# Expert loop of a hybrid block: weights in 1-MB transfers, a written TensorE order, a silu gate, and 34 weight places

## The chip, the cores and the metric

The kernel runs on one core of one Trainium2 chip. The metric is the device time of one launch in microseconds (us), the median of several runs. The engines are TensorE (PE in the rows; PEld is its weight load), VectorE (DVE), ScalarE (ACT), GpSimd (POOL) and SyncE (SP), which only issues DMAs here. Sixteen DMA engines carry every transfer of the core.

## The reference, cut to what matters

One layer over 1,024 positions of width 1,024. The first two thirds of the kernel's time (projections, a short convolution, attention, output projection) are not touched. The change is in the mixture of experts at the end: each token goes to 2 of 32 experts.

```python
comb = jnp.sum(jax.nn.one_hot(e_idx, N_EXPERTS, dtype=jnp.float32)
               * w_k[..., None], axis=-2).astype(h.dtype)
out = jnp.zeros_like(h)
for e in range(N_EXPERTS):
    a = jax.nn.silu(h @ w_gate[e]) * (h @ w_up[e])
    out = out + comb[..., e:e + 1] * (a @ w_down[e])
```

`D_MODEL` is 1024 and `D_EXPERT` 256, so an expert has 3 MB of float32 weights. The block's output is `x + gate2 * out`.

## The kernel before, in words

**One expert.** The loop in `moe` goes through 32 experts in a fixed order, each with up to 104 token rows (`CAP`). For expert number n, GpSimd gathers the rows of its tokens into a tile `xg` (L1198, an indirect DMA); TensorE transposes them in 8 instructions into `xT` (L1214); ScalarE and VectorE copy them out as `xf` (two eighths, plain float32) and `xh` and `xl` (six eighths, as a high and a low part; L1215 to L1217). `front` then makes `gu`, gate and up side by side, from 4 weight pieces: 4 matmuls with the first piece whole (L1224), 18 with the other three, each split into a high part by ScalarE (L1185) and a low part by VectorE (L1189). The gate is `sg`: a sigmoid on ScalarE, then two VectorE multiplications (L1237, L1238). TensorE transposes it (`aT`, L1241), and it is split in turn (`ah`, `al`). `back` makes `yp` from the 2 down pieces with 12 matmuls (L1260 to L1262), VectorE multiplies it by the token weights and by `gate2` into `y` (L1263), and GpSimd adds the rows to the output in DRAM by an indirect, accumulating DMA (L1264, here called the scatter).

**Order.** `front(n)` calls `back(n-1)` before the gate of n. Each engine takes its instructions in the order in which a scheduler, at build time, put them; `issue_after` forces one place in that order. Before the change, nothing forces TensorE's order in the loop. On the chip each engine works strictly in its order and waits on semaphores.

**Weights.** An expert has 6 pieces of 512 KB (128 partitions of 4 KB): 192 pieces in all, fetched by SyncE in order (L1105). `plan_room` lists the places. Thirty-one are filled ahead (`fill`); of them 27 are used again in a ring, `wphi` being given back to the split parts. `pa0` (also `stage`), `pa1`, `H0`, `H1` and `H2` are blocks of 4 neighbouring places; the others stand alone. When a piece is used up, `piece_done` issues the load of the next one into the next place of the ring. A fourth block under the name `H` is `xg`, 4 gather tiles, so gather n+4 waits for the transposes of n. `y` has 3 tiles.

**The start and the end of the loop.** The token tables (`tabi`, the rows of each expert; `tabw`, their weights) are made by routing code just ahead. Four GpSimd products `twts` (L997) belong to `tabw`. The scatters of the four neighbouring experts may be in flight together, since these have no token in common; only the last one waits for all. A loop for overflowing experts follows and has nothing to do with these inputs.

Of the kernel before, what the change touches and what calls it, by code (L numbers as in the profile page):

```python
# [56 lines left out]
def plan_room():  # L57
# [5 lines left out]
    fill = [t for t in RAW_ROOM for _ in range(ROOM[t])]  # L63
    ring = [t for t in fill if t not in SPLIT_ROOM]
    free = [(0.0, t) for t in SPLIT_ROOM if t not in fill for _ in range(ROOM[t])]
# [21 lines left out]
class Builder:  # L87
# [978 lines left out]
    def raw_begin(self):  # L1066

        a = self.a
        self.order = [8 * g + e for e in range(8) for g in range(4)]
        gu = [[a["w_gu"][e, q] for q in range(4)] for e in self.order] + [[]]  # L1070
        wd = [[]] + [[a["w_d"][e, q] for q in range(2)] for e in self.order]
        self.pieces = [p for g, w in zip(gu, wd) for p in g + w]
        self.fill, self.ring, self.pairs = plan_room()
        self.raws, self.nraw, self.nsplit, self.npiece, self.blocks = [], 0, 0, 0, {}
        self.raw_fill("wpraw", "wphi", "wplo", "pa0")

    def raw_fill(self, *slots):

        while self.nraw < len(self.fill) and self.fill[self.nraw] in slots:
            self.raw_next()  # L1080

    def raw_rest(self, late):
# [5 lines left out]
        self.xg, self.rows = [xg[:, i, :] for i in range(4)], {}  # L1088
# [4 lines left out]
        self.raw_fill("H2")  # L1093

    def raw_next(self):
        if self.pieces:
            self.raws.append(self.raw_load(self.pieces.pop(0)))

    def raw_load(self, src):

        i = self.nraw
        self.nraw += 1
        fill, ring = self.fill, self.ring
        raw = self.piece_tile(fill[i] if i < len(fill) else ring[(i - len(fill)) % len(ring)], list(src.shape), F32)
        self.nc.sync.dma_start(out=raw, in_=src)  # L1105
        return raw

    def piece_tile(self, slot, shape, dt):

        if slot in ("pa0", "pa1", "H0", "H1", "H2"):  # L1110
            if slot not in self.blocks:
                if slot == "pa0":
                    t = self.stage_tile[:, 0:4 * D].rearrange("p (n d) -> p n d", n=4)
                else:
                    pool, tag = (self.hp, "H") if slot[0] == "H" else (self.mgp, slot)
                    t = pool.tile([P, 4, D], dt, name=slot, tag=tag)
                self.blocks[slot] = [t, 0]
            t, n = self.blocks[slot]
            self.blocks[slot][1] = (n + 1) % 4
            t = t[:, n, :]  # L1120
            return t.rearrange("p (k n) -> p k n", k=2) if len(shape) == 3 else t
        pool = self.wk if slot == "mhi" else self.wp if slot in ("wphi", "wplo") else self.mgp
        return pool.tile(shape, dt, name=slot, tag=slot, bufs=ROOM[slot])

    def moe(self):
        tc, nc, a = self.tc, self.nc, self.a
        with ExitStack() as ctx:
# [7 lines left out]
            self.gate2 = gate2  # L1135
            self.adds = []
            job = None
            for n, e in enumerate(self.order):
# [16 lines left out]
            with tc.For_i(0, cnt, 1) as i:  # L1155
# [6 lines left out]
                job = self.front(NE, P, tabo[:, 0:1],  # L1162
                                 [a["w_gu"][ds(e, 1), q].rearrange("o p k n -> p (o k) n") for q in range(4)])
                self.back(NE, P, *job, tabo[:, 1:2].bitcast(F32),
                          [a["w_d"][ds(e, 1), q].rearrange("o p n -> p (o n)") for q in range(2)])
# [5 lines left out]
    def piece_done(self, src):  # L1171
# [3 lines left out]
        if src is None and (i >= len(self.fill) or self.fill[i] in self.ring):  # L1175
            self.raw_next()
# [27 lines left out]
    def front(self, n, m, idx, wgu_src, between=None):  # L1204
# [12 lines left out]
        nc.vector.tensor_tensor(out=xl, in0=ps[:, nw:KC, 0:m], in1=xh.bitcast(F32), op=ALU.subtract)  # L1217
        gu = pp.tile([P, 512], F32, name="gu", tag="gu")[0:m, :]
        for q in range(4):
            ks = range(2 * q, 2 * q + 2)  # L1220
            if q in WHOLE:
                w = self.whole(wgu_src[q])
                for kc in ks:
                    nc.tensor.matmul(gu, xf[:, kc, :], w[:, kc % 2, :], start=(kc == 0), stop=False)  # L1224
                self.piece_done(wgu_src[q])
                continue
            w = self.piece(wgu_src[q])
            for kc in ks:
                wh, wl = (t[:, kc % 2, :] for t in w)
                nc.tensor.matmul(gu, xh[:, kc - nw, :], wh, start=(kc == 0), stop=False)  # L1230
                nc.tensor.matmul(gu, xh[:, kc - nw, :], wl, start=False, stop=False)
                nc.tensor.matmul(gu, xl[:, kc - nw, :], wh, start=False, stop=(kc == KC - 1))
        s = wk.tile([P, 256], F32, name="sg")[0:m, :]
        if between:
# [99 lines left out]
```

## Time and profile before

| what | value |
|---|---|
| time, median of 3 runs | 1232.86 us (1231.57 to 1232.97) |
| the profiled execution, its own time | 1234.61 us |
| its span, first to last instruction | 1232.6 us |
| TensorE busy in the span | 1124.1 us (91%) |
| TensorE's mean granted clock | 0.973 of full speed |
| first product of the expert loop | 848.5 us into the span |
| first product of the last expert (number 31) | 1200.49 us |

The span is what the rows below are counted in; the execution's own time is 2.0 us longer, and lies 1.75 us above the median. The stretch of about 385 us from 848 on is the expert loop, and 32 us of it are behind the last expert's first product.

### The profile page before, as it was taken

What the parts mean: (1) busy time and instruction counts of PE and PEld (TensorE: products, weight loads), DVE (VectorE), ACT (ScalarE), POOL (GpSimd) and SP (SyncE); (2) the same over time, 40 slices, a digit from 0 to 9 for tenths busy, and PEclk for the clock granted to TensorE, in tenths of its full rate; (3) what the DMA queues carried; (4) which work ended last, traced back from release to release, by engine and by line L of the source; (5) the groups of instructions that cost most, each with busy time, mean ns of one, the idle gap of its engine ahead of it and who ended that gap; (6) DMA issues with size and microseconds to landing.
All of it is one profiled execution on the core that took longest, in us unless ns stands there. A gap on an engine that the chain in (4) does not pass through costs nothing. (4 is left out here: it accounts for less than half of the span.)

```text
span 1232.6 us, 15836 instructions
## 1 busy us (share of the span) xinstructions
PE 1124.1 (91%) x5428; PEld 884.5 (72%) x5428; DVE 814.6 (66%) x1505; ACT 558.8 (45%) x939; POOL 327.9 (27%) x307
## 2 busy tenths in 40 slices
PE   4889999999999989999999999985999998898893
PEld 4878888898997767788888888873666665565562
DVE  5956565565565655645666656867888887586782
ACT  5544553543543664333232233334665565464560
POOL 4440320230230210000000102645465444243211
PEclk9999999999999999999999999996999999899897
DMA  8514123122211426655656564387999999999941
GB/s 306 187 53 126 35 78 81 48 65 71 71 52 43 112 78 201 206 182 175 216 190 205 188 253 188 121 323 218 293 297 294 285 310 272 323 302 293 317 151 25
DMA packets 75219, 222.93 MB, mean 181 GB/s; under 512 B 12897, under 2 KB 17601, under 8 KB 75138
## 3 DMA queue, kind: packets, MB, share of 16 engines
q1 hardware_dynamic: 64162, 200.64, 49.5%
q0 software_dynamic: 9824, 17.09, 6.5%
q10 hardware_dynamic: 1152, 4.19, 0.9%
q8 instruction: 43, 0.70, 0.2%
q14 instruction: 38, 0.31, 0.1%
HBM read 201.57 MB, written 26.58 MB: 185 GB/s over the span
## 5 line engine op out<-in xcount | busy, mean ns | idle before, releaser
L1198 POOL DMA_INDIRECT xg<-d_h,tabi x32 | 78.7, 2459 | 153.3 <-PE xT L1214 92.4
L436 POOL TENSOR_SCALAR p<-p,su 128x128 f32<-128x128 f32 (+3 forms) x64 | 48.6, 765 | 229.4 <-DVE su L435 208.4
L498 PE MATMUL gps<-hhi,wphi 128*128 128x512 f32 x256 | 101.6, 397 | 0.6 <-ACT wphi L99 0.6
L500 PE MATMUL gps<-hhi,wplo 128*128 128x512 f32 x256 | 101.3, 396 | 0.5 <-DVE wplo L100 0.5
L99 ACT ACTIVATE wphi<-wpraw 128x1024 fp32r<-128x1024 f32 x42 | 44.6, 1063 | 125.0 <-PE gps L499 47.5
L499 PE MATMUL gps<-hlo,wphi 128*128 128x512 f32 x256 | 101.2, 395 | 0.0
L450 DVE TENSOR_TENSOR pl<-pT,ph 128x512 fp32r<-128x512 f32 (+1 forms) x96 | 51.2, 552 | 46.8 <-ACT ph L449 46.4
L498 PE MATMUL cps<-hhi,wphi 128*128 128x512 f32 x192 | 77.4, 403 | 2.4 <-ACT wphi L99 2.0
L1264 POOL DMA_INDIRECT out_dram<-y,tabi x32 | 59.0, 1842 | 66.5 <-DVE y L1263 47.2
L499 PE MATMUL cps<-hlo,wphi 128*128 128x512 f32 x192 | 76.3, 398 | 0.0
L500 PE MATMUL cps<-hhi,wplo 128*128 128x512 f32 x192 | 75.1, 399 | 0.3 <-DVE wplo L100 0.3
L449 ACT ACTIVATE ph<-pT 128x512 fp32r<-128x512 f32 (+1 forms) x96 | 44.5, 489 | 64.3 <-PE pT L446 58.9
L100 DVE TENSOR_TENSOR wplo<-wpraw,wphi 128x1024 fp32r<-128x1024 f32 x42 | 51.4, 1224 | 31.3 <-ACT wphi L99 31.3
L186 DVE SCALAR_TENSOR_TENSOR adaw<-adaw,cb 128x1024 f32<-128x1024 f32 x32 | 39.2, 1225 | 47.1 <-DMA adaw<-in_w_ada_dram 47.1
L1185 ACT ACTIVATE wphi<-H 128x1024 fp32r<-128x1024 f32 x48 | 50.2, 1058 | 42.8 <-issue 30.3
L316 PE MATMUL qkvp<-wplo,hhi 128*128 128x384 f32 x192 | 65.7, 342 | 0.7 <-DVE wplo L100 0.7
L315 PE MATMUL qkvp<-wphi,hhi 128*128 128x384 f32 x192 | 65.4, 348 | 0.8 <-ACT wphi L99 0.8
L317 PE MATMUL qkvp<-wphi,hlo 128*128 128x384 f32 x192 | 65.2, 340 | 0.0
L100 DVE TENSOR_TENSOR wplo<-waraw,wphi 128x768 fp32r<-128x768 f32 (+2 forms) x37 | 38.0, 1027 | 40.0 <-ACT wphi L99 39.1
L816 POOL IOTA slots<- 128x128 f32 x1 | 0.2, 244 | 226.9 <-DVE adaw L186 226.9
L434 ACT ACTIVATE p<-p,m 128x128 f32<-128x128 f32 (+3 forms) x64 | 49.4, 773 | 22.9 <-DVE m L431 13.1
L498 PEld LDWEIGHTS gps<-hhi,wphi 128*128 128x128 f32 x256 | 48.1, 188 | 12.7 <-ACT wphi L99 1.1
(473 smaller groups left out, 3211.2 us busy)
## 6 DMA issues: line engine op xcount, KB each, us to landing
H<-in_w_gu_dram SPq DMA_DIRECT2D x53, 512.0 KB
adaw<-in_w_ada_dram SPq DMA_DIRECT2D x32, 512.0 KB
wpraw<-in_w_g_dram SPq DMA_DIRECT2D x30, 512.0 KB
H<-in_w_d_dram SPq DMA_DIRECT2D x30, 512.0 KB
stage<-in_w_gu_dram SPq DMA_DIRECT2D x22, 512.0 KB
wplo<-in_w_gu_dram SPq DMA_DIRECT2D x18, 512.0 KB
pa<-in_w_gu_dram SPq DMA_DIRECT2D x18, 512.0 KB
ld<-in_w_ada_dram SPq DMA_DIRECT2D x16, 512.0 KB
```

What stands on the lines that cost most here:

```text
L100: (lo_eng or nc.vector).tensor_tensor(out=lo, in0=raw, in1=hi.bitcast(F32), op=ALU.subtract)
L315: nc.tensor.matmul(ps, hi[:, kc, sl], wh, start=(kc == 0), stop=False)
L316: nc.tensor.matmul(ps, hi[:, kc, sl], wl, start=False, stop=False)
L317: nc.tensor.matmul(ps, lo[:, kc, sl], wh, start=False, stop=(kc == KC - 1))
L434: nc.scalar.activation(pr, pr, AF.Exp, bias=m[:, b:b + 1], scale=-1.0, accum_out=su)
L450: nc.vector.tensor_tensor(out=pl[:, off:], in0=tp[:, off:], in1=ph[:, off:].bitcast(F32), op=ALU.subtract)
L498: nc.tensor.matmul(ps, wh, hi[:, kc, :], start=(kc == 0), stop=False)
L499: nc.tensor.matmul(ps, wh, lo[:, kc, :], start=False, stop=False)
L500: nc.tensor.matmul(ps, wl, hi[:, kc, :], start=False, stop=(kc == KC - 1))
L1185: nc.scalar.activation(hi, raw, AF.Copy)
L1198: self.gather = self.nc.gpsimd.indirect_dma_start(out=x[0:m, :], out_offset=None, in_=self.d_h2, in_offset=bass.IndirectOffsetOnAxis(ap=id ...
L1264: ins = nc.gpsimd.indirect_dma_start(out=self.out, out_offset=bass.IndirectOffsetOnAxis(ap=idx, axis=0), in_=y, in_offset=None, bounds_che ...
```

## The change

Six things change together in the expert loop. (1) Two neighbouring places of a block are filled by one 1-MB transfer, and `layout` puts both pieces of it side by side, so that a partition gets 8 KB in one row. Single places still get 512 KB. (2) There are 34 places, 30 of them in the ring: `xg` keeps 2 gather tiles and gives the other half as block `H3`, and the place `wkx` stands where the third `y` tile was. A load is issued when the place, or both places, of it are used up. (3) `in_turn` forces TensorE's order: the first piece's products of n, the gate transposes of n-1, the other products of n, all 8 row transposes of n+1, `back(n-1)`. (4) The gate is one ScalarE instruction (Silu) and one VectorE instruction, which also applies the token weights; `y` then multiplies by `gate2` alone. (5) Gather n+1 is written in `between`, and gather n waits for the transposes of n-2. (6) The last scatter waits only for the one four before it, like the others. Numbers of lines move: 1105 to 1106 (1-MB) and 1131 (512 KB), 1198 to 1248, 1214 to 1265, 1224 to 1291, 1241 to 1316, 1263 to 1338, 1264 to 1339.

```diff
-ROOM = {"mhi": 3, "row": 2, "mh": 1, "ml": 1, "wpraw": 3, "wphi": 4, "wplo": 4,
-        "pa0": 4, "pa1": 4, "H0": 4, "H1": 4, "H2": 4}
-RAW_ROOM = ("wphi", "pa0", "wpraw", "wplo", "pa1", "H0", "H1", "H2")
-SPLIT_ROOM = ("mhi", "row", "mh", "ml", "wphi")
+
+RAW_ROOM = (("wphi", 4), ("pa0", 4), ("wpraw", 2), ("wplo", 4), ("pa1", 4), ("H0", 4), ("H1", 4), ("H2", 4),
+            ("H3", 2), ("wpraw", 1), ("wkx", 1))
+SPLIT_ROOM = {"mhi": 3, "row": 2, "mh": 1, "ml": 1, "wphi": 4}
+BLOCKS = {"pa0": 4, "pa1": 4, "H0": 4, "H1": 4, "H2": 4, "H3": 2}
+ROOM = SPLIT_ROOM | {"wpraw": 3, "wplo": 4, "wkx": 1}
...
-        gu = [[a["w_gu"][e, q] for q in range(4)] for e in self.order] + [[]]
-        wd = [[]] + [[a["w_d"][e, q] for q in range(2)] for e in self.order]
-        self.pieces = [p for g, w in zip(gu, wd) for p in g + w]
+        gu = [[a["w_gu"][e, q] for q in range(2)] for e in self.order] + [[]]
+        wd = [[]] + [[a["w_d"][e]] for e in self.order]
+        self.twos = [p for g, w in zip(gu, wd) for p in g + w]
...
-        self.xg, self.rows = [xg[:, i, :] for i in range(4)], {}
+        self.blocks["H3"] = [xg, 0]
+        self.xg, self.rows = [xg[:, i, :] for i in (2, 3)], {}
...
+        self.raw_fill("H2", "H3", "wpraw")
+
+    def raw_next(self, limit):
+
+        i, two = self.nraw, self.slot_of(self.nraw) in BLOCKS
+        if i >= NCHUNK or i + two >= limit:
+            return False
+        src = self.twos[i // 2]
+        if two:
+            t, n = self.block(self.slot_of(i))
+            self.nc.sync.dma_start(out=t[:, n:n + 2, :].rearrange("p a n -> p (a n)"),
+                                   in_=src if len(src.shape) == 2 else src.rearrange("p k n -> p (k n)"))
+            self.raws += [self.view(t[:, n + b, :], src) for b in range(2)]
+            self.blocks[self.slot_of(i)][1] = (n + 2) % BLOCKS[self.slot_of(i)]
+            self.nraw += 2
+        else:
+            self.raws.append(self.raw_load(self.half(src, i % 2)))
+        return True
...
+            self.raw_fill("wkx")
...
+            self.turn = None
+            xs = self.tokens(0, CAP, self.tabi[:, self.order[0]:self.order[0] + 1])
...
+                following = []
+
+                def before():
+                    if n > 0:
+                        jobs[-1] += self.turned(n, CAP, acts)
+
+                def between():
+                    if n < NE - 1:
+                        f = self.order[n + 1]
+                        following.append(self.tokens(n + 1, CAP, self.tabi[:, f:f + 1]))
+                    if n > 0:
+                        self.back(n - 1, CAP, *jobs[-1], [None] * 2)
+                acts = self.front(n, CAP, *xs[1:], self.tabw[:, e:e + 1], [None] * 4, before, between)
+                jobs.append([xs[0]])
+                xs = following[0] if following else None
+            self.back(NE - 1, CAP, *jobs[-1], *self.turned(NE - 1, CAP, acts), [None] * 2)
...
-        if src is None and (i >= len(self.fill) or self.fill[i] in self.ring):
-            self.raw_next()
+        if src is None and self.slot_of(i) in self.ring:
+            self.nfree += 1
+            while self.raw_next(len(self.fill) + self.nfree):
+                pass
...
-            x = self.xg[n % 4]
+            x = self.xg[n % 2]
...
-        for kc in range(KC):
-            nc.tensor.transpose(ps[:, kc, 0:m], x[0:m, kc * P:(kc + 1) * P], self.ident[0:m, 0:m])
+        with self.in_turn(n) as turn:
+            for kc in range(KC):
+                turn(nc.tensor.transpose(ps[:, kc, 0:m], x[0:m, kc * P:(kc + 1) * P], self.ident[0:m, 0:m]))
         nc.scalar.activation(xf, ps[:, 0:nw, 0:m], AF.Copy)
         nc.scalar.activation(xh, ps[:, nw:KC, 0:m], AF.Copy)
         nc.vector.tensor_tensor(out=xl, in0=ps[:, nw:KC, 0:m], in1=xh.bitcast(F32), op=ALU.subtract)
+        return idx, nw, xf, xh, xl
...
+    @contextmanager
+    def in_turn(self, n):
+
+        def turn(ins):
+            self.turn = ins if n < NE else None
+        with ExitStack() as ctx:
+            if n < NE and self.turn is not None:
+                ctx.enter_context(self.tc.issue_after(self.turn.ins))
+            yield turn
...
-                for kc in ks:
-                    nc.tensor.matmul(gu, xf[:, kc, :], w[:, kc % 2, :], start=(kc == 0), stop=False)
+                with self.in_turn(n) as turn:
+                    for kc in ks:
+                        turn(nc.tensor.matmul(gu, xf[:, kc, :], w[:, kc % 2, :], start=(kc == 0), stop=False))
                 self.piece_done(wgu_src[q])
+                if before and q == 0:
+                    before()
...
+            with self.in_turn(n) as turn:
+                for kc in ks:
+                    wh, wl = (t[:, kc % 2, :] for t in w)
+                    nc.tensor.matmul(gu, xh[:, kc - nw, :], wh, start=(kc == 0), stop=False)
+                    nc.tensor.matmul(gu, xh[:, kc - nw, :], wl, start=False, stop=False)
+                    turn(nc.tensor.matmul(gu, xl[:, kc - nw, :], wh, start=False, stop=(kc == KC - 1)))
         s = wk.tile([P, 256], F32, name="sg")[0:m, :]
+        nc.scalar.activation(s, gu[:, 0:256], AF.Silu)
+        nc.vector.scalar_tensor_tensor(s, gu[:, 256:512], comb[0:m, :], s, op0=ALU.mult, op1=ALU.mult)
         if between:
...
-        nc.scalar.activation(s, gu[:, 0:256], AF.Sigmoid)
-        nc.vector.tensor_tensor(out=s, in0=gu[:, 0:256], in1=s, op=ALU.mult)
-        nc.vector.tensor_tensor(out=s, in0=gu[:, 256:512], in1=s, op=ALU.mult)
...
-        return idx, ah, al
...
+        return ah, al
...
-        comb = comb[0:m, :]
         wd = [self.piece(wd_src[q]) for q in range(2)]
-        y = wk.tile([P, D], F32, name="y", bufs=3 if n < NE else 1)[0:m, :]
+        y = wk.tile([P, D], F32, name="y", bufs=2 if n < NE else 1)[0:m, :]
         yp = pp.tile([P, D], F32, name="yp", tag="yp", bufs=1)[0:m, :]
...
-        nc.vector.scalar_tensor_tensor(y, yp, comb, self.gate2[0:m, :], op0=ALU.mult, op1=ALU.mult)
+        with self.in_turn(n) as turn:
...
+        nc.vector.tensor_tensor(out=y, in0=yp, in1=self.gate2[0:m, :], op=ALU.mult)
...
-        if n < NE - 1:
+        if n < NE:
             befores = self.adds[-4:-3] or self.out_init
             self.adds.append(self.unordered(ins, self.adds[-3:], befores, "experts of other groups have other tokens"))
-        elif n == NE - 1:
-            self.after(ins, self.adds[-4:], "the last sum waits for all")
+        else:
...
-        "w_gu": np.concatenate([f["w_gate"][0], f["w_up"][0]], axis=2).reshape(NE, 4, 2, P, 512)
+        "w_gu": np.concatenate([f["w_gate"][0], f["w_up"][0]], axis=2).reshape(NE, 2, 4, P, 512)
         .transpose(0, 1, 3, 2, 4),
-        "w_d": f["w_down"][0].reshape(NE, 2, P, D),
+        "w_d": f["w_down"][0].reshape(NE, 2, P, D).transpose(0, 2, 1, 3).reshape(NE, P, 2 * D),
```

The first place at which the order moves is GpSimd's queue at the start of the loop. Before (`xg` is a gather, `twts` a product of the token weights, `d_tab` a record for overflowing experts):

```order
L1198 DMA xg<-d_h_95,tabi 104x1024
L997 TENSOR_TENSOR twts<-tval_7686,fae_7560 128x96 x2
L997 TENSOR_TENSOR twts<-tval_7686,fbe_7569 128x96 x2
L1198 DMA xg<-d_h_95,tabi 104x1024 x3
L1025 DMA d_tab<-rec_90,idx_89 65536x2 x2
L1048 IOTA jidx 128x1
```

After the change:

```order
L999 TENSOR_TENSOR twts<-tval_7675,fae_7549 128x96 x2
L999 TENSOR_TENSOR twts<-tval_7675,fbe_7558 128x96 x2
L1248 DMA xg<-d_h_95,tabi 104x1024 x2
L1050 IOTA jidx 128x1
L1248 DMA xg<-d_h_95,tabi 104x1024 x3
L1027 DMA d_tab<-rec_90,idx_89 65536x2 x2
```

The first gather stood ahead of the four `twts` products and now stands behind them; two of the gathers stand ahead of the first `jidx`.

The second place is TensorE's queue around one change of experts, in the steady part of the loop. Before:

```order
L1260 MATMUL yp<-row,ah 104x512
L1261 MATMUL yp<-mhi,ah 104x512
L1262 MATMUL yp<-row,al 104x512
L1214 MATMUL xT<-ident,xg 128x104 x6
L1241 MATMUL aT<-ident,sg 128x104 x2
L1224 MATMUL gu<-stage,xf 104x512 x2
L1230 MATMUL gu<-row,xh 104x512
L1231 MATMUL gu<-mhi,xh 104x512
L1260 MATMUL yp<-wphi,ah 104x512
L1261 MATMUL yp<-mhi,ah 104x512
L1232 MATMUL gu<-row,xl 104x512
L1230 MATMUL gu<-row,xh 104x512
```

After the change, where the rows left out are ten more `yp` products like their neighbours:

```order
L1301 MATMUL gu<-mh,xh 104x512
L1302 MATMUL gu<-wphi,xl 104x512
L1265 MATMUL xT<-ident,xg 128x104 x8
L1335 MATMUL yp<-mhi,ah 104x512
...
L1335 MATMUL yp<-mhi,ah 104x512
L1336 MATMUL yp<-ml,ah 104x512
L1337 MATMUL yp<-mhi,al 104x512
L1291 MATMUL gu<-wplo,xf 104x512 x2
L1316 MATMUL aT<-ident,sg 128x104 x2
L1300 MATMUL gu<-row,xh 104x512
L1301 MATMUL gu<-row,xh 104x512
```

The last 6 row transposes stood directly ahead of the gate transposes and of the first products that use them. Now all 8 stand ahead of the 12 `yp` products, and the gate transposes stand behind the first products of the next expert.

The third place is SyncE's queue in the same part. Before (128x1024 is a piece of 512 KB):

```order
L1105 DMA H_7526<-in_w_d_dram 128x1024 x2
L1105 DMA H_7526<-in_w_gu_dram 128x1024 x2
L1105 DMA H_7536<-in_w_gu_dram 128x1024
L1105 DMA H_7521<-in_w_gu_dram 128x1024
L1105 DMA H_7536<-in_w_d_dram 128x1024 x2
L1105 DMA stage<-in_w_gu_dram 128x1024 x3
L1105 DMA H_7536<-in_w_gu_dram 128x1024
L1105 DMA wpraw<-in_w_d_dram 128x1024 x2
L1105 DMA wpraw<-in_w_gu_dram 128x1024
```

After the change (128x2048 is 1 MB; L1131 issues the single places):

```order
L1106 DMA pa_7414<-in_w_gu_dram 128x2048
L1106 DMA H_7515<-in_w_d_dram 128x2048
L1106 DMA H_7518<-in_w_gu_dram 128x2048 x2
L1106 DMA H_7524<-in_w_d_dram 128x2048
L1106 DMA xg<-in_w_gu_dram 128x2048
L1131 DMA wpraw<-in_w_d_dram 128x1024
L1106 DMA H_7524<-in_w_gu_dram 128x2048
L1131 DMA wkx<-in_w_d_dram 128x1024
L1106 DMA stage<-in_w_gu_dram 128x2048
```

Most pairs of pieces are now one entry; the pieces come in the same sequence.

## Rows read from the trace of the kernel before

**Rows 1.** The page: span and busy time.

```profile
span 1232.6 us, 15836 instructions
...
PE 1124.1 (91%) x5428; PEld 884.5 (72%) x5428; DVE 814.6 (66%) x1505; ACT 558.8 (45%) x939; POOL 327.9 (27%) x307
```

**Rows 2.** Busy time by stretch of the expert loop; columns in the first line.

```profile
core 0: us, PE busy (x) PEld busy (x) DVE busy (x) ACT busy (x) POOL busy (x), PEclk, DMA share, GB/s
880.00:920.00 40.00, 37.33 (x163) 24.70 (x163) 32.98 (x38) 23.82 (x35) 28.11 (x14) 1.00 1.02 307
...
1040.00:1080.00 40.00, 31.78 (x117) 19.81 (x116) 25.48 (x30) 18.68 (x27) 12.11 (x6) 0.83 0.98 308
...
1120.00:1160.00 40.00, 32.02 (x133) 20.41 (x132) 26.44 (x30) 19.10 (x27) 11.98 (x6) 0.91 0.95 294
...
1185.00:1190.00 5.00, 4.08 (x25) 3.01 (x24) 4.79 (x7) 4.21 (x7) 0.00 (x0) 1.00 0.21 53
```

**Rows 3.** Waits of TensorE, 860 to the end: us in total, times, longest.

```profile
PE gu L1224 <- ACT xf L1215: 18.7, 27, 1.2
PE aT L1241 <- DVE sg L1238: 15.8, 14, 5.3
```

**Rows 4.** Waits of SyncE's DMA queue from 800 on: us in total, times, longest.

```profile
SPq L1105 <- DMA H<-in_w_gu_dram: 51.8, 33, 3.1
...
SPq L1105 <- DVE mhi L1189: 20.0, 15, 2.8
```

**Rows 5.** The DMA view of 820 to 845, in 40 slices of 0.625 us.

```profile
GB/s 419 419 426 406 406 419 420 419 413 419 420 406 216 229 315 184 275 269 295 406 419 426 413 420 419 420 413 157 0 0 0 0 0 0 0 13 0 66 59 157
```

**Rows 6.** Timeline of SyncE's queue: start, us to the last issue of the group, x issues.

```profile
904.31 0.33 SPq L1105 DMA_DIRECT2D H<-in_w_gu_dram  x1
...
1162.99 7.17 SPq L1105 DMA_DIRECT2D H<-in_w_gu_dram  x4
1171.73 4.19 SPq L1105 DMA_DIRECT2D H<-in_w_d_dram  x4
1176.83 0.33 SPq L1105 DMA_DIRECT2D H<-in_w_gu_dram  x1
```

**Rows 7.** Indirect DMAs issued from 904 to 1163: count, median us to landing.

```profile
xg<-d_h,tabi POOLq DMA_INDIRECT x23, 10.6
out_dram<-y,tabi POOLq DMA_INDIRECT x23, 10.9
```

**Rows 8.** Timeline of GpSimd at the start of the loop.

```profile
841.24 1.30 POOL L1198 DMA_INDIRECT xg<-d_h,tabi  x1 [1.37 <-DVE ee L1007]
842.58 0.67 POOL L997 TENSOR_TENSOR twts<-tval,fae 128x96 bf16<-128x96 bf16 x2
843.22 1.71 POOL L997 TENSOR_TENSOR twts<-tval,fbe 128x96 bf16<-128x96 bf16 x2
```

**Rows 9.** Timeline of TensorE: first product of expert 5 and of expert 15.

```profile
902.31 0.68 PE L1224 MATMUL gu<-H,xf 128*104 128x512 f32 x1 [0.93 <-ACT xf L1215]
...
1009.15 0.68 PE L1224 MATMUL gu<-stage,xf 128*104 128x512 f32 x1 [0.45 <-ACT xf L1215]
```

**Rows 10.** Groups of instructions: mean ns of one splitting instruction on ScalarE and on VectorE.

```profile
L1185 ACT ACTIVATE wphi<-H 128x1024 fp32r<-128x1024 f32 x48 | 50.2, 1058 | 42.8 <-issue 30.3
...
L1189 DVE TENSOR_TENSOR mhi<-H,wphi 128x1024 fp32r<-128x1024 f32 x27 | 33.0, 1221 | 11.8 <-PE gu L1231 9.7 <-PE gu L1232 1.4 <-ACT wphi L1185 0.5
```

**Rows 11.** Timeline of the end: TensorE (expert 31), then the last scatter on GpSimd.

```profile
1200.49 1.96 PE L1224 MATMUL gu<-H,xf 128*104 128x512 f32 x4 [0.45 <-ACT xf L1215]
...
1206.69 0.40 PE L1232 MATMUL gu<-wphi,xl 128*104 128x512 f32 x1
...
1210.89 0.46 PE L1260 MATMUL yp<-wphi,ah 128*104 128x512 f32 x1 [1.29 <-DVE y L1263]
...
1213.51 0.40 PE L1262 MATMUL yp<-wphi,al 128*104 128x512 f32 x1
...
1217.89 1.61 POOL L1264 DMA_INDIRECT out_dram<-y,tabi  x1 [5.25 <-issue]
```

More of the change, by code (lines that the diff above doesn't have):

```diff
@@ L1 @@
-from contextlib import ExitStack
+from contextlib import ExitStack, contextmanager
 import numpy as np
@@ L57, in plan_room @@
 def plan_room():
-    fill = [t for t in RAW_ROOM for _ in range(ROOM[t])]
+    fill = [t for t, n in RAW_ROOM for _ in range(n)]
     ring = [t for t in fill if t not in SPLIT_ROOM]
-    free = [(0.0, t) for t in SPLIT_ROOM if t not in fill for _ in range(ROOM[t])]
+    free = [(0.0, t) for t, n in SPLIT_ROOM.items() if t not in fill for _ in range(n)]
     pairs, split, done = [], 0.0, 10.0
@@ L1099, in raw_load, with half, view, slot_of @@
+    def half(self, src, b):
+        return src[:, b * D:(b + 1) * D] if len(src.shape) == 2 else src[:, 2 * b:2 * b + 2, :]
+    def view(self, t, src):
+        return t if len(src.shape) == 2 else t.rearrange("p (k n) -> p k n", k=2)
+    def slot_of(self, i):
+        n = len(self.fill)
+        return self.fill[i] if i < n else self.ring[(i - n) % len(self.ring)]
     def raw_load(self, src):
-        i = self.nraw
+        raw = self.piece_tile(self.slot_of(self.nraw), list(src.shape), F32)
@@ L1102, in raw_load, with block @@
         self.nraw += 1
-        fill, ring = self.fill, self.ring
-        raw = self.piece_tile(fill[i] if i < len(fill) else ring[(i - len(fill)) % len(ring)], list(src.shape), F32)
         self.nc.sync.dma_start(out=raw, in_=src)
         return raw
-    def piece_tile(self, slot, shape, dt):
[L1110 to L1119, printed above, removed]
+    def block(self, slot):
+        if slot not in self.blocks:
+            if slot == "pa0":
+                t = self.stage_tile[:, 0:4 * D].rearrange("p (n d) -> p n d", n=4)
+            else:
+                pool, tag = (self.hp, "H") if slot[0] == "H" else (self.mgp, slot)
+                t = pool.tile([P, 4, D], F32, name=slot, tag=tag)
+            self.blocks[slot] = [t, 0]
+        return self.blocks[slot]
@@ L1202, in gather_rows, with tokens @@
         return self.rows[n]
-    def front(self, n, m, idx, wgu_src, between=None):
+    def tokens(self, n, m, idx):
         nc, wk, pp = self.nc, self.wk, self.pp
@@ L1217, in front @@
         nc.vector.tensor_tensor(out=xl, in0=ps[:, nw:KC, 0:m], in1=xh.bitcast(F32), op=ALU.subtract)
+        return idx, nw, xf, xh, xl
[7 more added lines that the diff above has]
+            yield turn
+    def front(self, n, m, nw, xf, xh, xl, comb, wgu_src, before=None, between=None):
+        nc, wk, pp = self.nc, self.wk, self.pp
         gu = pp.tile([P, 512], F32, name="gu", tag="gu")[0:m, :]
@@ L1239, in front @@
         ps = pp.tile([P, 256], F32, name="aT", tag="aT")
[L1240 to L1243 removed]
+        with self.in_turn(n) as turn:
+            for j in range(2):
+                turn(nc.tensor.transpose(ps[:, j * P:j * P + m], s[:, j * P:(j + 1) * P], self.ident[0:m, 0:m]))
@@ L1266, in back @@
                                            compute_op=ALU.add)
-        if n < NE - 1:
+        if n < NE:
             befores = self.adds[-4:-3] or self.out_init
             self.adds.append(self.unordered(ins, self.adds[-3:], befores, "experts of other groups have other tokens"))
-        elif n == NE - 1:
-            self.after(ins, self.adds[-4:], "the last sum waits for all")
+        else:
+            self.after(ins, self.adds[-4:], "behind the sums of the main loop")
 def layout(inputs):
```

59 lines of the change are left out of this document (27 added, 32 removed).

## The prediction

> **What bounds the loop now.** I read the page first: TensorE is busy 91% of the span [rows 1], which suggests that TensorE sets the time. In the loop that holds only in part, so the next view is the busy time by stretch, from which one stretch is to be compared with another: from 880 on the DMA engines' share is 0.95 to 1.02 in every stretch shown up to 1160, and 0.21 near 1190, while TensorE is busy 37.3 of 40 us in one stretch and only 31.8 and 32.0 of 40 in two others, where its clock is 0.83 and 0.91 [rows 2]. So there are two regimes. Up to expert 15 the loop has a period: ten experts take 1009.15 − 902.31 = 106.8 us, 10.68 us each [rows 9]. At that pace expert 31 would begin at 1009.15 + 16 × 10.68 = 1180.0; it begins at 1200.49 [rows 11]. These 20.4 us are lost to starvation: the weights in the places are used up, and TensorE stands at the gate transposes, up to 5.3 us at once [rows 3]; behind such a stop the rows show a lower granted clock.
>
> Why the weights are late is told by SyncE: its issues wait mostly for earlier transfers of its own (51.8 us in the largest of several such groups), and much less for a place to come free (20.0 us) [rows 4]. From 904.31 to 1162.99 it issues 123 pieces, 2.10 us each [rows 6], 12.6 us for the six of an expert, against the 10.68 that TensorE takes. In 820 to 833, with no gather or scatter in flight, the same 512-KB transfers run at 419 GB/s [rows 5], 1.25 us a piece. The difference, 258.7 − 123 × 1.25 = 105 us, is what 23 gathers and 23 scatters in that time [rows 7] cost the DMA engines: 4.6 us a pair. Behind the last gathers, from 1162.99 to 1176.83, it is 8 pieces in 13.84 us [rows 6], 1.73 each; with about 1.3 scatters in that time, one scatter costs (13.84 − 10.0) / 1.3 = 2.9; half a pair is 2.3. I take 2.6.
>
> So the end hangs on the last weight piece. It is issued at 1176.83 [rows 6], 13.84 us behind the eighth before it, whose place in SyncE's own limit it takes; with the same flight it lands about 1190, where the DMA share is down to 0.21 [rows 2].
>
> **The change, part by part.**
>
> *TensorE's order.* In the steady part TensorE waits for `xf` directly behind the row transposes, 0.93 us at one expert and 0.45 at another [rows 9], 18.7 us in 27 waits [rows 3], 0.69 each. With 12 `yp` products between (1210.89 to 1213.51 for twelve of them [rows 11], about 2.9 us with the last) that wait is covered; the gate transposes get the same cover. TensorE's own period becomes about 10.0. VectorE was busy 33.0 of 40 us [rows 2] and has one gate instruction less, so it does not bind. On the end this is worth nothing by itself while the weights set it: a faster TensorE uses its stock sooner and starves sooner.
>
> *Start.* Gather 0 stood ahead of the four `twts` products and now stands behind them: 0.67 + 1.71 = 2.38 us [rows 8] later, and with it the first product and everything that waits for a place: +2.3 for the last landing.
>
> *Three places more.* From 837 to 845 the DMA engines are nearly idle, 0 to 66 GB/s in a slice [rows 5]. Three pieces more fit there and leave the loaded part: −3 × 1.25 = −3.8. Two gather tiles in place of four, and two `y` tiles, cost nothing as long as a gather is in time: gather n now goes out behind the transposes of n−2, two periods (20 us) ahead of its use, and needs about 2.5 us on GpSimd and 10.6 to land [rows 7]. The cover is 7 us.
>
> *Scatters ahead of the last piece.* TensorE will be nearer to the weights when the last piece lands, about two experts further along than before at that time, so two more scatters lie ahead of it: +2 × 2.6 = +5.2 (4.6 to 5.8).
>
> *1-MB transfers.* No row of before has one. From below: nothing, since the bytes and the DMA engines are the same and several transfers are in flight anyway. From above: if twice the bytes in flight filled the share from 0.97 to 1.00 over 904 to 1177, 3% of 273 us, 8 us. I take −2, near the lower end, since 0.95 to 1.02 leaves little idle and 512 KB already run at 419 GB/s. [...]
>
> *The last sum.* Scatter 31 starts at 1217.89 after idling 5.25 us on GpSimd [rows 11]. Its `y` is ready about 2.6 us before that: the twelve products end at 1213.51 + 0.40 [rows 11], and `y`, by a VectorE instruction of like size [rows 10], takes 1.2 to 1.3 more: ready at 1215.2. That wait goes: −2.6, if the end is otherwise the same.
>
> *The sum.* Last landing: 1190 + 2.3 − 3.8 + 5.2 − 2 = 1191.7. From there: the last third-and-fourth pieces of gate and up of expert 31 land two pieces ahead of it (2 × 1.73 = 3.5), splitting takes 1.06 + 1.22 [rows 10], six products 1.4 (half of the twelve above), so `gu` ends at about +0.2. Before, from `gu`'s last product (begun at 1206.69, its result at about 1206.9 [rows 11]) to the last `yp` block are 4.0 us, and from there to the span's end 1232.6 − 1210.89 = 21.7, less 2.6. That is 0.2 + 4.0 + 19.1 = 23.3. TensorE will have stood before, and may run at the lower clock; a stretch with a clock of 0.83 loses 0.17 × 40 = 6.8 us [rows 2] over its stops, and I take 3 for one of them. Span: 1191.7 + 23.3 + 3 = 1218.0. The execution's own time is 2.0 us longer than the span, and the median 1.75 us below that execution: 1218.3, say **1218 us**.
>
> **The rivals.**
>
> *A. The DMA no longer sets the end.* If 1-MB transfers make the stream 3% faster, the sum falls by 6 more, to 1212. If they make it fast enough to keep ahead, TensorE sets the end: expert 15 begins at 1009.15 + 2.4 − 15 × 0.69 = 1001.2, expert 31 160 us later, and 32.1 − 2.6 behind it the span ends at 1190.7: about 1191. For: SyncE waits for its own transfers. Against: share near 1.00, and the gathers and scatters stay.
>
> *B. Nothing is gained.* The end follows the weights, and the three places are filled late or the clock takes it back: 1190 + 2.3 + 5.2 for the landing and 23.3 + 7 behind it give 1227.8, and with the last wait staying in another form 1230 to 1233. For: the bytes are the same. Against: the idle DMA slices before 845.
>
> *C. Slower: gathers come late.* With two tiles a gather has two periods. If transfers twice as large in flight hold its rows up, landing takes 21 us in place of 10.6; with 2.5 on GpSimd, 23.5 us for two experts, 11.75 a period. 31 periods are 364 us against 352 before (848.5, in the table of times, to 1200.49): expert 31 begins 12 + 2.4 later, 2.6 comes back, 1245. It decides from a landing of about 20 us on. For: the DMA engines are full, and nothing sets a gather before a weight. Against: a gather lands in 10.6 us [rows 7] while eight pieces take 13.84 [rows 6], so its rows do not stand behind all that is in flight.
>
> **How the numbers follow.** The forecast, weights setting the end within 1212 to 1226, gets 0.64; A 0.15, two thirds of it below 1209; B 0.13; C 0.08. Leaving out A's lower part and C gives 1209 to 1231 for 8 in 10. A measurement can tell about 0.2% (2.5 us) from no change. Faster: 0.64 + 0.15 + 0.05 of B = 0.84; same 0.08; slower 0.08.
>
> **What will show it.** First product of expert 0 near 851; period near 10.0 with no waits for `xf`; DMA share near 1.0 from about 870 on; starvation earlier than expert 16; last landing near 1192; expert 31's last `yp` near 1199; last scatter directly behind `y`. Wrong would be: a DMA stream of clearly under 2.1 us a piece (A), waits of the row transposes for gathers (C), or places that load only behind 848 (B).

## The result and the profile after

The changed kernel takes 1218.99 us, median of 4 runs (1217.8 to 1220.57), against 1232.91 for the kernel before: a ratio of 0.9886, with a 95% interval of 0.9867 to 0.9905. The forecast was 1218 (1209 to 1231). The sum came out; two of its steps did not, and their errors nearly cancel, so the hit to 1 us is in part luck. That is what the rest is about.

The page after, span and busy time:

```profile
span 1215.7 us, 15701 instructions
...
PE 1118.8 (92%) x5428; PEld 887.8 (73%) x5428; DVE 799.9 (66%) x1473; ACT 558.5 (46%) x937; POOL 311.6 (26%) x307
```

The span is 16.9 us shorter than before. TensorE's busy time fell by only 5.3 us of 1124.1 [rows 1], so most of the gain is less waiting. This profiled execution took 1217.8 us and is the fastest of the four, 1.2 us below their median.

Busy time by stretch (columns as in [rows 2]):

```profile
880.00:920.00 40.00, 40.00 (x190) 27.64 (x189) 35.46 (x39) 27.88 (x39) 18.33 (x13) 1.00 1.02 322
1040.00:1080.00 40.00, 32.49 (x141) 22.10 (x140) 29.04 (x31) 22.69 (x31) 13.66 (x7) 0.91 0.97 317
1120.00:1160.00 40.00, 32.43 (x146) 22.15 (x144) 24.96 (x27) 19.55 (x27) 17.77 (x8) 0.96 0.98 343
1160.00:1200.00 40.00, 36.83 (x150) 24.77 (x150) 29.89 (x34) 22.05 (x32) 8.55 (x4) 0.91 0.41 115
1180.00:1185.00 5.00, 5.00 (x28) 3.80 (x27) 3.85 (x5) 5.00 (x8) 1.23 (x1) 1.00 0.32 72
1185.00:1190.00 5.00, 5.00 (x21) 3.05 (x20) 5.00 (x7) 2.66 (x5) 1.39 (x1) 1.00 0.02 6
```

From 880 to 920 TensorE is busy without a gap, where it was at 37.3 of 40 us before [rows 2]. In two later stretches it is at 32.5 and 32.4, little more than before (31.8 and 32.0). The last weights have landed by 1185, where the DMA share has fallen from 0.32 to 0.02; in the trace's packet records the last weight packet ends at 1183.1 (at 1189.7 in the kernel before).

Waits of TensorE from 860 on:

```profile
PE yp L1335 <- ACT ah L1320: 9.2, 2, 4.7
PE yp L1335 <- DVE y L1338: 7.7, 3, 5.2
PE yp L1335 <- ACT xh L1267: 7.5, 1, 7.5
PE gu L1291 <- ACT xf L1266: 2.4, 2, 2.1
```

The 27 waits for `xf` [rows 3] are down to 2. What is left is eight waits. Four of them are long, 4.5 to 7.5 us (at 1011, 1050, 1126 and 1161 us), and these four are starvation although the engine named is ScalarE or VectorE: ahead of each, a split on ScalarE had itself waited 8.6 to 9.7 us for a weight piece. The other four are 0.3 to 2.1 us long. The clearest long one is at expert 28. TensorE there (start, us, what, and the idle time before it):

```profile
1149.97 1.88 PE L1291 MATMUL gu<-pa,xf 128*104 128x512 f32 x4
...
1161.60 0.75 PE L1335 MATMUL yp<-wphi,ah 128*104 128x512 f32 x1 [4.68 <-ACT ah L1320]
...
1166.85 2.10 PE L1291 MATMUL gu<-H,xf 128*104 128x512 f32 x4
...
1176.62 1.88 PE L1291 MATMUL gu<-H,xf 128*104 128x512 f32 x4
...
1186.20 1.88 PE L1291 MATMUL gu<-stage,xf 128*104 128x512 f32 x4
```

and ScalarE at the same time:

```profile
1149.51 1.06 ACT L1235 ACTIVATE wphi<-H 128x1024 fp32r<-128x1024 f32 x1 [0.71 <-ACT xh L1267]
1160.26 1.06 ACT L1235 ACTIVATE wphi<-H 128x1024 fp32r<-128x1024 f32 x1 [9.69 <-DMA H<-in_w_gu_dram]
1161.22 0.33 ACT L1320 ACTIVATE ah<-aT 128x208 fp32r<-128x208 f32 x1
```

Three things are to be seen. First, ScalarE stands 9.69 us for a piece of gate and up of the next expert, split ahead of need, and `ah`, which TensorE needs at once, stands behind that split in ScalarE's order, though the gate transposes that it reads had ended at 1152.03; as soon as the piece is there, `ah` follows (1161.22), then the `yp` products (1161.60). Second, this is the last such stop: from 1166.85 two experts take 9.77 and 9.58 us, close to TensorE's own period of 9.59. Third, expert 31 begins at 1186.20, 29.5 us before the span's end.

The start of the loop, on GpSimd, on SyncE's queue and on TensorE:

```profile
839.89 1.63 POOL L999 TENSOR_TENSOR twts<-tval,fbe 128x96 bf16<-128x96 bf16 x2
841.73 1.21 POOL L1248 DMA_INDIRECT xg<-d_h,tabi  x1 [0.21 <-DVE ra L1013]
```

```profile
842.19 0.33 SPq L1164 DMA_DIRECT2D gate<-d_row  x1
842.62 0.37 SPq L1131 DMA_DIRECT2D wkx<-in_w_d_dram  x1
```

```profile
849.72 1.62 PE L1265 MATMUL xT<-ident,xg 104*128 104x104 f32 x8 [7.91 <-DMA xg<-d_h,tabi]
851.77 3.74 PE L1291 MATMUL gu<-wphi,xf 128*104 128x512 f32 x4 [0.43 <-ACT xf L1266]
```

The first gather goes out at 841.73, 0.5 us later than before [rows 8], but its rows are used only at 849.72, 8.0 us behind its issue. Two 512-KB transfers (`gate2`'s row and the place `wkx`) are issued 0.5 and 0.9 us behind it.

The end, on GpSimd:

```profile
1196.80 1.61 POOL L1339 DMA_INDIRECT out_dram<-y,tabi  x1 [5.87 <-DVE al L1321]
1201.23 1.61 POOL L1339 DMA_INDIRECT out_dram<-y,tabi  x1 [2.82 <-DVEq L1201]
```

Scatter 31 follows scatter 30 by 4.43 us, against 6.85 before (1211.04 and 1217.89).

### The profile page after: what moved, and what is told of

It reads as the page before. It is cut to its first block, busy times and chain, and to the rows that moved or that the text cites. A ratio compares the mean times of both kernels' runs of the same rounds, so it can differ in the third digit from the quotient of the medians.

```text
span 1215.7 us, 15701 instructions
## 1 busy us (share of the span) xinstructions
PE 1118.8 (92%) x5428; PEld 887.8 (73%) x5428; DVE 799.9 (66%) x1473; ACT 558.5 (46%) x937; POOL 311.6 (26%) x307
## 5 line engine op out<-in xcount | busy, mean ns | idle before, releaser
L1339 POOL DMA_INDIRECT out_dram<-y,tabi x32 | 82.6, 2581 | 156.7 <-DVE y L1338 132.7
L102 DVE TENSOR_TENSOR wplo<-wpraw,wphi 128x1024 fp32r<-128x1024 f32 x42 | 51.4, 1224 | 30.0 <-ACT wphi L101 29.9
L1235 ACT ACTIVATE wphi<-H 128x1024 fp32r<-128x1024 f32 x39 | 41.1, 1060 | 42.1 <-DMA H<-in_w_gu_dram 26.7
L1248 POOL DMA_INDIRECT xg<-d_h,tabi x32 | 41.3, 1292 | 63.2 <-PE xT L1265 59.6
L502 PEld LDWEIGHTS gps<-hhi,wplo 128*128 128x128 f32 x256 | 48.1, 188 | 12.4 <-DVE wplo L102 0.7
```

The lines of the kernel that those rows point to most:

```text
L102: (lo_eng or nc.vector).tensor_tensor(out=lo, in0=raw, in1=hi.bitcast(F32), op=ALU.subtract)
L502: nc.tensor.matmul(ps, wl, hi[:, kc, :], start=False, stop=(kc == KC - 1))
L1339: ins = nc.gpsimd.indirect_dma_start(out=self.out, out_offset=bass.IndirectOffsetOnAxis(ap=idx, axis=0), in_=y, in_offset=None, bounds_che ...
```

## The experiments

"Loop" is the time from the first product of expert 0 to that of expert 31 in the profiled execution; it leaves out what happens ahead of the loop, where the first product lay between 846 and 856 us in these profiles. "Lost" is what the loop holds beyond 31 median periods of the kernel, counting periods more than 0.3 us over the median. Each ratio is to runs of the kernel before that were made alongside, whose median lay between 1232.9 and 1235.0 us, so kernels compare better by ratio than by median. In order_gate_only and order_gate_y_first more than half of the periods are themselves lengthened by waits; against 9.6 us an expert they lose 64.5 and 57.4 us. Two parts of the change, the gate (4) and the new place of the gather (5), were not run by themselves.

| kernel | median, us | ratio to before, 95% interval | period, us | lost, us | loop, us |
|---|---|---|---|---|---|
| before | 1232.9 | 1 | 10.73 | 20.4 | 352.0 |
| the change | 1219.0 | 0.9886 (0.9867 to 0.9905) | 9.59 | 36.8 | 334.4 |
| order_gate_only | 1242.8 | 1.0057 (1.0031 to 1.0084) | 11.28 | 33.5 | 362.1 |
| singles_34 | 1223.3 | 0.9915 (0.9888 to 0.9942) | 9.68 | 42.4 | 341.0 |
| no_forced_order | 1232.1 | 0.9968 (0.9948 to 0.9988) | 10.56 | 24.5 | 344.7 |
| last_wait_back | 1220.8 | 0.9890 (0.9864 to 0.9917) | 9.59 | 38.1 | 335.3 |
| two_places_32 | 1226.8 | 0.9937 (0.9915 to 0.9958) | 9.60 | 47.2 | 344.4 |
| spread_104 | 1207.4 | 0.9787 (0.9761 to 0.9813) | 9.60 | 29.4 | 326.9 |
| spread_112 | 1187.2 | 0.9624 (0.9593 to 0.9655) | 9.66 | 6.2 | 306.0 |
| before_spread_112 | 1213.0 | 0.9831 (0.9805 to 0.9857) | 10.77 | 0.5 | 333.8 |
| order_gate_y_first | 1233.9 | 1.0000 (0.9980 to 1.0020) | 10.68 | 38.6 | 355.0 |
| spread_112_no_order | 1208.0 | 0.9786 (0.9756 to 0.9815) | 10.59 | 6.3 | 327.3 |
| spread_112_singles | 1179.4 | 0.9556 (0.9532 to 0.9580) | 9.66 | 3.6 | 303.0 |
| spread_112_start | 1183.3 | 0.9572 (0.9547 to 0.9597) | 9.66 | 8.2 | 307.6 |

**1. Order, gate and last wait alone (order_gate_only).** The changed kernel with 31 places, four gather tiles, three `y` tiles and 512-KB transfers:

```diff
-            ("H3", 2), ("wpraw", 1), ("wkx", 1))
+            ("wpraw", 1))
...
-        i, two = self.nraw, self.slot_of(self.nraw) in BLOCKS
+        i, two = self.nraw, False
...
```

> The changed kernel with 512-KB transfers everywhere and 31 places (4 gather tiles, 3 y tiles): what is left of the change is TensorE's order, the gate and the last scatter's wait. Theory W (the weights set the end, as in the prediction): the shorter period earns next to nothing, the end moves by the last wait (-2.6) and little else: 1228 to 1231 us. Rival P (TensorE's period sets the end): nearly the whole gain is here already, 1219 to 1221.

Measured 1242.8: slower than both kernels, outside what either theory gave. Experts 2 to 9 run at 9.6 us, so the order does shorten the period; then starvation sets in earlier, and from expert 18 on a wait appears that neither theory had. Waits of TensorE:

```profile
PE yp L1334 <- DVE y L1337: 28.6, 13, 7.8
PE gu L1290 <- ACT xf L1265: 15.3, 5, 6.9
```

and VectorE around one of them (`yp`'s first product, which has one PSUM tile for all experts, starts at 1162.89 after 1.65 us of waiting):

```profile
1157.54 1.23 DVE L1238 TENSOR_TENSOR mhi<-H,row 128x1024 fp32r<-128x1024 f32 x1 [0.42 <-PE gu L1300]
1158.99 1.22 DVE L1238 TENSOR_TENSOR ml<-H,wphi 128x1024 fp32r<-128x1024 f32 x1 [0.22 <-PE gu L1300]
1160.38 1.23 DVE L1238 TENSOR_TENSOR mh<-H,wphi 128x1024 fp32r<-128x1024 f32 x1 [0.17 <-PE gu L1300]
1161.53 1.22 DVE L1337 TENSOR_TENSOR y<-yp,gate 104x1024 f32<-104x1024 f32 x1
```

`y` of the expert before stands behind three splits in VectorE's order, where in the changed kernel it stands ahead of `al` for all but 9 experts. The change forces TensorE's order only; VectorE's is left to the scheduler, and it came out differently in this build.

**2. 512-KB transfers with 34 places (singles_34).** Only the second edit of experiment 1.

> The changed kernel with its 34 places and every transfer of 512 KB. Theory W: the three places earn 3 to 4 us over the kernel with 31 places, and 1-MB transfers 0 to 2 more, so 1219 to 1225 us here. Rival D (1-MB transfers speed up the stream or hide the lanes' limit): 1228 or more, as the gain comes with the size.

Measured 1223.3, as theory W said, with most of the gain there. The change's 1-MB transfers are worth 4.3 us on these medians (prediction: 2), but the two intervals overlap. The traces show what they do to the weights. The queue that carries them, in the 259 us from 904 to 1163 (packets, MB, share of the time of 16 engines), before, here, and in the change:

```profile
q1 hardware_dynamic: 17974, 64.92, 75.9%
```

```profile
q1 hardware_dynamic: 18178, 65.66, 74.5%
```

```profile
q1 hardware_dynamic: 12072, 68.73, 74.6%
```

The stream is about 5% faster with 1-MB transfers, 1.98 us for 512 KB against 2.07 here and 2.09 before, and the last weight packet ends at 1183.1 against 1189.4 here (one profile each).

**3. The scheduler's order again (no_forced_order).**

```diff
-            if n < NE and self.turn is not None:
+            if False:
```

> The changed kernel without TensorE's forced order (the scheduler's order again, gate, places and 1-MB transfers kept). Theory W: the period goes back to about 10.3 to 10.7 us, the weights last longer and starvation is less, so the end moves by at most 3 us: 1217 to 1222. Rival P: 31 x 0.7 to 1.1 us more, 1235 or more.

Measured 1232.1: between the two, and not what theory W said. The median period is back at 10.56 (experts 2 to 7 still run at 9.6), and TensorE waits for `xf` again:

```profile
PE gu L1291 <- ACT xf L1266: 31.1, 22, 4.3
```

Less is lost to starvation (24.5 for 36.8), so the weights give back part, but not all: the loop is 10.3 us longer, and the ratio moves by 0.0082, 10 us.

**4. The last wait back (last_wait_back).**

```diff
+        if n == NE - 1:
+            self.after(ins, self.adds[-4:], "the last sum waits for all")
...
```

> The changed kernel with the last scatter waiting for the four before it, as before the change. Prediction's term: +2.6 us, 1221.6. From the trace after (scatter 30 at 1196.8, and 6.85 us from one to the next in the trace before): +2.4, 1221.4. Rival: nothing, since the sums of the DMA end at the same time anyhow: 1219.

Measured 1220.8. The intervals overlap, so the median alone does not show it; the trace does. GpSimd, scatters 30 and 31:

```profile
1199.72 1.61 POOL L1339 DMA_INDIRECT out_dram<-y,tabi  x1 [6.02 <-DVE al L1321]
1206.63 1.61 POOL L1339 DMA_INDIRECT out_dram<-y,tabi  x1 [5.30 <-issue]
```

They are 6.91 us apart, against 4.43: the wait moves the last scatter by 2.5 us, as predicted (2.6).

**5. Two places fewer (two_places_32).**

```diff
-            ("H3", 2), ("wpraw", 1), ("wkx", 1))
+            ("wpraw", 1), ("wkx", 1))
...
```

With block `H3` gone, the kernel again has four gather tiles.

> The changed kernel with 32 places (block H3 gone, so again 4 gather tiles), all else kept, 1-MB transfers too. By the prediction's term of 1.25 us a place: 2.5 us slower than the change, 1221 to 1222. If the places are worth what the kernel with 31 places and 512-KB transfers showed against 34 (19 us for three): 1229 to 1233.

Measured 1226.8, between the two: 3.9 us a place by the medians and 3.1 by the ratios, not 1.25. Here too TensorE waits for `y` (34.6 us, 12 times), so this is the price of the places together with what the scheduler made of that build.

**6. Tokens spread over the rows (spread_104, spread_112, before_spread_112).** The table of tokens is made by comparing each token's rank within its expert with `slots`; other numbers in `slots` give the tokens other rows, and nothing else changes. For 112 rows:

```diff
-CAP = 104
+CAP = 112
...
         self.slots = iota("slots", [P, P], [[1, P]], 0, 0)
+        nc.gpsimd.iota(self.slots[:, 0:CAP].rearrange("p (a b) -> p a b", a=16), pattern=[[1, 16], [16, 7]], base=0,
+                       channel_multiplier=0, allow_small_or_imprecise_dtypes=True)
```

and for 104 rows with 8 runs of 13.

> The changed kernel; the tokens of an expert are given other rows of the 104: row 13*i+k takes the token of rank 8*k+i, so that the 45 to 101 real rows (empty rows move nothing) lie evenly over the eight runs of 13 rows. Theory U (a gather or scatter is cut into equal runs of rows, one run per DMA engine, so the real rows load only about 5 of 16 DMA engines and these set the pace of every weight piece): about 8 rows where 13 were, 2.4 us less per expert on the fullest engine (8 against 13 rows at 0.159 + 0.327 us each), little starvation left, 1183 to 1198 us. Rival M (the mean load of all 16 sets the pace): same rows, same bytes, 1217 to 1220.

> The changed kernel with 112 rows for an expert in place of 104 (16 runs of 7) and the tokens spread over the 16 runs. Theory U: about 4 real rows on each DMA engine, the weights no longer set the pace, TensorE's 9.6 us do: first product of expert 31 near 1152, 1180 to 1190 us. Rival M: 1217 to 1222.

> The kernel before, with the same two lines (112 rows, spread). Theory U: no starvation, TensorE's old period of 10.7 sets the end, 20.4 us come off: 1211 to 1215 us. Rival M: 1231 to 1236.

Measured 1207.4, 1187.2 and 1213.0. Rival M is out in all three: the same bytes cost much less. The kernel before loses almost nothing any more (0.5 us for 20.4), and lands where theory U put it. spread_112 is inside its range, spread_104 is not. How theory U shares the rows out among the DMA engines is an assumption: no run shows which engine carried which row. Its packet times are measured, in the kernel before: a 4-KB packet took 0.159 us in a gather by itself and 0.327 at the median on the indirect queue in the loop (most rows of the last scatters, with no weights in flight, also took 0.328). With the 8 rows that it assumes on the fullest engine they give an estimate of 6 × 1.25 + 8 × 0.486 = 11.4 us an expert, still over TensorE's 9.6, so starvation had to stay; the range was not worked out from them. With 4 rows it is 7.5 + 1.9 = 9.4. The estimate is rough. In spread_104 an expert's weights took 11.5 us from 904 to 1140, which fits; but with 13 rows it gives 13.8, and the weights took 12.6 in the kernel before and 11.9 in the change.

The gather itself shows it too. DMA view with no weights in flight, 40 slices, first the kernel before (842 to 845.15, slices of 0.079 us, 49 of the 53 packets of 4 KB of gather 0), then spread_112_start (844 to 848, slices of 0.1 us; the first burst is gather 0, the second belongs to gather 1):

```profile
GB/s 0 104 0 0 0 0 0 0 0 0 0 0 0 0 1 159 157 0 104 0 0 104 0 156 0 104 0 52 52 104 208 52 260 52 260 52 260 52 260 104
```

```profile
GB/s 0 0 0 0 0 0 0 0 0 0 0 0 0 0 0 0 0 0 0 205 164 287 41 246 205 369 246 287 83 42 0 0 82 164 205 205 164 328 287 206
```

By the packet records, the 53 rows of gather 0 move between 843.23 and 845.69 before, 2.5 us with at most 8 rows in flight at once; spread, the same 53 move between 845.97 and 847.09, 1.1 us with up to 18 in flight. Spreading also puts the rows into other partitions of the gather tile and of `y`, and no run separates that from what it does on the DMA engines. The busy time by stretch of spread_112:

```profile
880.00:920.00 40.00, 40.00 (x184) 28.43 (x183) 35.63 (x39) 27.13 (x37) 19.00 (x13) 1.00 1.00 285
1000.00:1040.00 40.00, 40.00 (x189) 28.55 (x188) 36.17 (x39) 27.90 (x38) 16.12 (x9) 1.00 1.03 364
1040.00:1080.00 40.00, 39.21 (x179) 27.69 (x178) 33.34 (x36) 26.47 (x39) 21.66 (x8) 1.00 1.03 371
```

The share is 1.00 to 1.03, much as it was in the kernel before (0.95 to 1.02 [rows 2]). In the two later stretches it moves 364 and 371 GB/s, where the two later stretches of that moved 308 and 294 [rows 2]; in the first, at the same share, it moves 285, where that moved 307. TensorE's waits from 860 on, and in before_spread_112 those of SyncE's queue:

```profile
PE gu L1293 <- ACT xf L1268: 2.4, 2, 2.1
PE yp L1337 <- DVE y L1340: 2.0, 2, 1.2
PE yp L1337 <- ACT ah L1322: 1.5, 1, 1.5
```

```profile
SPq L1107 <- DVE mhi L1191: 87.4, 54, 2.8
...
SPq L1107 <- DVE sg L1239: 22.8, 20, 1.3
SPq L1107 <- DVE ml L1191: 22.0, 20, 2.8
SPq L1107 <- DMA H<-in_w_gu_dram: 15.9, 17, 1.9
```

SyncE now waits for places (`mhi`, the splits that free them), no longer mostly for its own transfers [rows 4].

**7. `y` forced ahead of `al` (order_gate_y_first).** On the kernel of experiment 1:

```diff
-        nc.vector.tensor_tensor(out=al, in0=pv, in1=ah.bitcast(F32), op=ALU.subtract)
+        with ExitStack() as ctx:
+            if self.last_y is not None and n < NE:
+                ctx.enter_context(self.tc.issue_after(self.last_y.ins))
+            nc.vector.tensor_tensor(out=al, in0=pv, in1=ah.bitcast(F32), op=ALU.subtract)
...
```

> The kernel with 31 places and 512-KB transfers (order, gate, last wait), with y forced ahead of the next al on VectorE. Theory Y (in that kernel, from expert 18 on, the build-time order put y behind three splits, and the yp products, which have one PSUM tile, waited 1.65 to 2.04 us an expert for it, with a lower clock behind): those waits go and starvation alone sets the end, 1222 to 1230 us. Rival S (the three places less starve TensorE just as long): 1237 to 1243.

Measured 1233.9, between the two, and the edit did not do what it was for: it moved `al` behind `y`, and `y` still stands behind the splits (TensorE waits 2.04 us for it at experts 20, 23 and 26). How much of the 19.5 us between 31 and 34 places is `y` and how much the places stays open.

**8. The order where weights are in time (spread_112_no_order).** The edit of experiment 3 on spread_112.

> The kernel with 112 rows spread over the DMA engines, without TensorE's forced order. Theory: where the weights no longer bind, the order earns its whole size, 0.9 to 1.0 us an expert for some 25 experts: 1207 to 1215 us. Rival (the order is hidden here too): 1186 to 1192.

Measured 1208.0: 20.8 us slower than spread_112 (20.0 by the ratios), period 10.59 for 9.66, and the waits for `xf` are back:

```profile
PE gu L1293 <- ACT xf L1268: 17.9, 21, 2.1
```

**9. 512 KB where weights are in time (spread_112_singles).** The second edit of experiment 1 on spread_112.

> The kernel with 112 rows spread over the DMA engines, with all transfers of 512 KB. Theory: 1-MB transfers earned 4 us (1223.3 to 1219.0) by packets of 8 KB that take a little less time on the fullest DMA engine; where it no longer binds they earn nothing: 1185 to 1190 us. Rival (they earn by fewer issues, or by places filled sooner): 1190 to 1194.

Measured 1179.4, below both ranges, and the fastest kernel of the study. The loop is 3.0 us shorter than with 1-MB transfers (303.0 for 306.0). The rest, some 5 us, lies ahead of the loop, where the first product is at 846.0 for 855.8 in the two profiles. Of these 9.8 us, 2.8 are the gather, which takes 3.5 us from issue to use in place of 6.3 (next experiment); the other 7.0 are there when the gather is issued, and why was not settled. The change and last_wait_back, alike up to there, differ by 2.1 us at the first product (851.77 and 853.82).

**10. The first gather alone (spread_112_start).** On spread_112, with the `al` edit of experiment 7, and:

```diff
...
+            late = [self.wkx_load, nc.sync.dma_start(out=gate2, in_=src.to_broadcast([P, D]))]
+            for ins in late:
+                self.after(ins, [self.gather], "the first gather goes ahead")
```

> The kernel with 112 rows spread over the DMA engines; y forced ahead of the next al, and the loads of the place wkx and of gate2 wait for the first gather. Theory G (the first gather took 8.0 us to land against 5.2 before, since those two 512-KB transfers, issued half a microsecond behind it, shared the DMA engines with it): first product 2 to 3 us earlier, 1183 to 1185.5 us. Rival (the gather is late for its own issue): 1186 to 1188.

The two loads are also written behind the gather. Measured 1183.3, in theory G's range; the interval just overlaps that of spread_112. The loop is 1.5 us longer than in spread_112 (307.6 for 306.0), so the gain lies ahead of it. The trace shows the step itself. First gather on GpSimd and first transposes on TensorE, spread_112:

```profile
847.33 1.15 POOL L1250 DMA_INDIRECT xg<-d_h,tabi  x1 [0.17 <-DVE ra L1015]
```

```profile
853.63 1.72 PE L1267 MATMUL xT<-ident,xg 112*128 112x112 f32 x8 [6.18 <-DMA xg<-d_h,tabi]
```

and with the two transfers held back:

```profile
844.11 1.15 POOL L1252 DMA_INDIRECT xg<-d_h,tabi  x1 [0.17 <-DVE ra L1015]
```

```profile
847.68 1.73 PE L1269 MATMUL xT<-ident,xg 112*128 112x112 f32 x8 [3.44 <-DMA xg<-d_h,tabi]
```

6.3 us from issue to use became 3.6, as theory G had it. The gather was also issued 3.2 us earlier in this profile, which theory G does not explain.

## Why the prediction was right, point by point

*What bounds the loop.* Two regimes, an even pace of TensorE and then starvation: right, and starvation earlier than expert 16 was right too (expert 15). **"So the end hangs on the last weight piece" failed.** The last piece lands at 1183.1, 8.6 us earlier than the forecast 1191.7, and TensorE, busy without a gap from 1180 to 1190, does not stand for it: the end is set by the last stop (expert 28, over at 1166.85), then TensorE's own periods (9.77 and 9.58), then 29.5 us. The rows of before said so already: there the last piece landed 10 us ahead of expert 31's first product [rows 2, 11]. The sum from the landing on gave 26.3 us (with 3 for the clock) where 32.6 passed, although the 3 us did not show: the granted clock from 1180 to 1190 was 1.00. The two errors, 8.6 and 6.3 us, leave the forecast span of 1218.0 us 2.3 above the profiled 1215.7; that the median lies 3.3 us above this profile's span, and not 0.3, takes back the rest. To that extent the hit is luck.

*Order.* Period "about 10.0": 9.59. "Worth nothing by itself": half right. With 31 places it gave nothing (experiment 1, clouded by `y`'s place in that build), but taken out of the change it costs 10 us (experiment 3). Likely reasons, not shown one by one, are that behind the last stop every expert counts at the period, and that a faster TensorE frees places and sends scatters sooner. Where the weights are in time it is worth some 20 us (experiment 8).

*Start.* +2.3 for the four `twts` products: the first product came 3.2 us later (851.77 for 848.55), but the gather was issued only 0.5 us later than before. The gather's landing took 8.0 us, since `gate2`'s row and the new place `wkx` were being filled at that moment (experiment 10, which held back both on spread_112: 6.3 us became 3.6).

*Three places.* Mis-sized: 1.25 us a place, the time of one unloaded transfer [rows 5], where two places measured 7.8 us by the medians and 6.3 by the ratios (experiment 5), `y`'s place in VectorE's order included.

*1-MB transfers.* Mis-sized on the landing: −2, where the last weight packet ended 6.3 us earlier than with 512 KB (experiment 2); the 4.3 us that the term lacked are half of the 8.6 us by which the forecast landing was late. On the time it was 4.3 us with overlapping intervals, and the opposite sign once the rows are spread (experiment 9).

*The last wait.* −2.6 against 2.5 between the last two scatters in the trace: right there; on the time it is within the noise (experiment 4).

*Rivals.* A was named as "the DMA no longer sets the end", 1191 us; experiment 6 reached 1187, by another way than larger transfers. A's sign, a stream clearly under 2.1 us a piece, showed in part (1.98), but starvation stayed. In C a gather lands late: 13.0 us at the median in the change against the 20 from which it decides, so no. The price of 4.6 us for a gather and a scatter was right as a sum, but it is no fixed price of the bytes: spreading the same rows took 12 and 32 us off the change and about 20 off the kernel before (experiment 6). That the fullest DMA engines make it, and not the mean, was theory U's assumption: the sign of all three spread runs agrees, but no run shows the rows of each engine.

## What to carry to other kernels

A busy share near 1.0 did not say here that the DMA engines moved all they could: 0.95 and 0.98 went with 294 and 308 GB/s in the kernel before [rows 2], 1.03 with 364 and 371 in spread_112. When indirect DMAs run beside a stream, ask where the real rows lie among the empty ones; renumbering them cost one instruction and eight empty rows more, and brought 32 us. And find the last stop of the pacing engine before summing to the end: behind it that engine's own period counts, and what lands later without being waited for counts for nothing.

## What the runs showed of the hardware

In the kernel before, a gather of 104 rows, of which 53 moved 4 KB each, took 2.5 us for them, 88 GB/s, where weights came at 419 [rows 5]; with the same rows spread over 112 it took 1.1 us (experiment 6, spread_112_start: at most 8 rows in flight at once before, 18 spread). Spreading over 8 runs of 13 (spread_104) took 12 us off the change, over 16 runs of 7 (spread_112) 32 us. Which engine carried which row was not read directly, so how a gather is shared out among the DMA engines stays open.
